# Top-10 indices of rows: a batch's store moved behind the last exponentials, quarter parts in shared buffers, ranks written into the table of the exactness test

One core of one Trainium2 chip. The metric is the device time of one execution in microseconds (us), lower is better.

## The reference

For each of 8192 rows of 8192 random numbers, the column indices of the ten largest, in falling order of value:

```python
def reference(x, k):                      # x: 8192 x 8192 float32, k = 10
    indices = np.argpartition(x, -k, axis=1)[:, -k:]
    values = np.take_along_axis(x, indices, axis=1)
    sorted_idx = np.argsort(-values, axis=1)
    return np.take_along_axis(indices, sorted_idx, axis=1)
```

## The kernel before

The rows are worked off in 64 tiles of 128 rows, 4 MB each. A tile goes through these stations:

1. *load* (SyncE's queue): four pieces of 1 MB; the first tile has eight and the last nine smaller ones.
2. *exponentials* (ScalarE): exp(36 (x - 4.7)) in bf16, in two halves; in four quarters for tiles 61 and 62; in eight parts for tile 63.
3. *sums* (TensorE, "s" in the profile): wide matmuls of 512 columns add the exponentials up in groups.
4. *choice* (VectorE, "wall" and "cidb"): the groups with the largest sums.
5. *gather* (GpSimd, "cand") and *mask* (half on GpSimd, half on VectorE, "masked"): the candidates of the chosen groups.
6. *extraction* (TensorE, "g"): 24 narrow fp32 matmuls a tile, 8 columns or (tiles 61 to 63) 16.
7. *rank* (VectorE, "t8a", "t8b", "posb").
8. For each batch of tiles *finish*: VectorE steps, then *moves* on TensorE ("fo"), a copy and a store.

The parts that matter here, with cuts marked:

```python
epool = ctx.enter_context(tc.tile_pool(name="e", bufs=3))      # exponentials
...
def part(h, s0, n):                                # one half or quarter of a tile
    e = epool.tile([P, N // 2], bf16, tag="e", name="e")   # always a whole buffer
    nc.scalar.activation(out=e[:, 0:n * W], in_=xts[t][:, s0 * W:(s0 + n) * W], ...)
    # ... n * W / 512 wide matmuls read e
...
for t in range(last - 1):                          # last = 63
    interleave(choose_steps(t), rank_steps(t - LAG) if t >= LAG else [])
    if t >= 1:
        spread(t - 1)                              # the masks
    gather(t, 0, G)
    if t < last - 2:
        run(weigh_steps(t + 1))                    # exponentials and sums
    if 1 <= t < last - 2:
        extract(t - 1)
    todo = {last - 5: 6, last - 4: TB, last - 3: TB}.get(t, 3)
    run(later[:todo])                              # steps of a batch's finish
    later = later[todo:]
    # ... a finished batch is added to `later`; load(t + 3)

a, b, c = last - 2, last - 1, last
run(later)
wb, wc = weigh_steps(b), weigh_steps(c)
run(wb[0:3])
extract(a - 1, 0, 6)
run(wb[3:4])
extract(a - 1, 6, G)
run(wc[0:4])
run(rank_steps(a - 2))
# ... masks of a, choice of b
extract(a, 0, 2)
run(wc[4:5])
extract(a, 2, 4)
run(wc[5:])
extract(a, 4, G)
run(rank_steps(a - 1))
# ... choice of c, extraction of b and c, ranks, two finishes, exactness test
```

Each engine works its instructions off in this order. A finish of batch 6 (seven tiles) is seven moves, 14 matmuls; they come before tile 61's sums in TensorE's order.

Of the kernel before, what the change touches and what calls it, by code (L numbers as in the profile page):

```python
# [1 line left out]

# [1 line left out]

# [5 lines left out]
P = 128  # L11
N = 8192
BANK = 512
KMAX = 10
G = 12
TB = 8
BETA = 36.0
# [3 lines left out]
BIG_NEG = -1e30  # L21
LAG = 3
TAIL = 3
PAD = 320



# [8 lines left out]
def kernel(  # L36
# [6 lines left out]
    nc = tc.nc  # L43
# [3 lines left out]
    ntiles = nrows // P  # L47

    fp32 = mybir.dt.float32
    fp16 = mybir.dt.float16  # L50
    bf16 = mybir.dt.bfloat16
# [5 lines left out]
    ACTF = mybir.ActivationFunctionType  # L57
# [5 lines left out]
    consts = ctx.enter_context(tc.tile_pool(name="consts", bufs=1))  # L63
    epool = ctx.enter_context(tc.tile_pool(name="e", bufs=3))
    small = ctx.enter_context(tc.tile_pool(name="small", bufs=2))
    bpool = ctx.enter_context(tc.tile_pool(name="batch", bufs=1))

    pad = ctx.enter_context(tc.tile_pool(name="pad", bufs=1)).tile([P, PAD], fp32, name="pad")
    nc.vector.memset(pad[:, 0:1], 0.0)
# [12 lines left out]
    last = ntiles - 1  # L82
# [5 lines left out]
    xts, ss, gs, idxs, cands, masked, batch = {}, {}, {}, {}, {}, {}, {}  # L88
    picked, ready = {}, {}

    def layout(t):
        return thin if t >= ntiles - TAIL else wide
# [8 lines left out]
    def parts(t):  # L101
        S = layout(t).S
        if t < ntiles - TAIL:
            return [S // 2] * 2
        return [S // 4] + [S // 8] * 5 + [S // 16] * 2 if t == last else [S // 4] * 4
# [25 lines left out]
    bias = consts.tile([P, 1], fp32)  # L131
# [3 lines left out]
    for lay, nsend in ((wide, TB), (thin, TAIL)):  # L135
        R, A, S = lay.R, lay.A, lay.S
# [8 lines left out]
        for s in range(S):  # L145
            nc.vector.tensor_copy(
                out=lay.group[:, s, :].rearrange("p (a s) -> p a s", s=S)[:, :, s],
                in_=lay.own_a,
# [8 lines left out]
    slots = consts.tile([P, G], fp16)  # L157
    nc.vector.tensor_copy(out=slots, in_=slots_i)
    wall = consts.tile([P, ntiles, 16], fp32)
    tall = consts.tile([P, ntiles], fp32)  # L160
    first_sum = np.cumsum([0] + [len(parts(t)) for t in range(ntiles)]).tolist()
    nsums = first_sum[-1]
    eall = consts.tile([P, nsums], fp32)
# [5 lines left out]
    def weigh_steps(t):  # L169
        lay = layout(t)  # L170
        S, W = lay.S, lay.W
        ss[t] = spsum.tile([P, wide.W], fp32, tag="s", name="s")[:, 0:W]

        def part(h, s0, n):
            e = epool.tile([P, N // 2], bf16, tag="e", name="e")
            nc.scalar.activation(  # L176
                out=e[:, 0:n * W], in_=xts[t][:, s0 * W:(s0 + n) * W],
                func=ACTF.Exp, bias=bias[:, 0:1], scale=BETA,
                accum_out=eall[:, first_sum[t] + h:first_sum[t] + h + 1],
            )  # L180
            for i in range(n):
                for j in range(0, W, BANK):
                    nc.tensor.matmul(sums[:, j:j + BANK], lhsT=lay.group[:, s0 + i, :],  # L183
                                     rhs=e[:, i * W + j:i * W + j + BANK],
                                     start=s0 + i == 0, stop=s0 + i == S - 1)

        sums, steps, s0 = ss[t], [], 0
        for h, n in enumerate(parts(t)):
            steps.append(lambda h=h, s0=s0, n=n: part(h, s0, n))
            s0 += n  # L190
        return steps
# [35 lines left out]
    def gather(t, g0, g1):  # L227
        if g0 == 0:
            cands[t] = small.tile([P, G, 16], fp32, tag="cand", name="cand")
        nc.gpsimd.add_instruction(  # L230
            mybir.InstIndirectCopy(
                name=nc.get_next_instruction_name(),
                ins=[nc.gpsimd.lower_ap(xts[t]), nc.gpsimd.lower_ap(idxs[t][:, g0:g1])],
                outs=[nc.gpsimd.lower_ap(cands[t][:, g0:g1].rearrange("p g s -> p (g s)"))],
                num_valid_indices=16 * (g1 - g0),
            )
        )
        if g1 == G:
            del xts[t], idxs[t]
# [15 lines left out]
    def spread(t):  # L255
        mask(nc.vector, t, 0, G // 2)
        mask(nc.gpsimd, t, G // 2, G)

    def extract(t, c0=0, c1=G):
        if c0 == 0:  # L260
            gs[t] = gpsum.tile([P, G * thin.R], fp32, tag="g", name="g")
        R = layout(t).R
        for c in range(c0, c1):
            nc.tensor.matmul(gs[t][:, c * R:(c + 1) * R],  # L264
                             lhsT=masked[t][:, c, :, :].rearrange("p a s -> p (a s)"),
                             rhs=layout(t).place, start=True, stop=True)

    def rank_steps(t):
        n = G * layout(t).R
        g = gs.pop(t)[:, 0:n]  # L270
        b = batch_of[t]
        pos = batch[b][1][:, t - starts[b], :]
        t8a = small.tile([P, 8], fp32, tag="t8a", name="t8a")
        t8b = small.tile([P, 8], fp32, tag="t8b", name="t8b")
        g2 = small.tile([P, G * thin.R], fp32, tag="g2", name="g2")[:, 0:n]
        return [
            lambda: nc.vector.max(out=t8a, in_=g),  # L277
            lambda: nc.vector.match_replace(out=g2, in_to_replace=t8a, in_values=g,  # L278
                                            imm_value=BIG_NEG),
            lambda: nc.vector.max_index(out=pos[:, 0:8], in_max=t8a, in_values=g),  # L280
            lambda: nc.vector.max(out=t8b, in_=g2),  # L281
            lambda: nc.vector.max_index(out=pos[:, 8:16], in_max=t8b, in_values=g2),  # L282
            lambda: nc.vector.tensor_copy(out=tall[:, t:t + 1],
                                          in_=t8b[:, KMAX - 9:KMAX - 8]),
        ]


# [67 lines left out]
        ]  # L355

    def interleave(*lists):
        for group_ in zip(*[l for l in lists if l]):
            for step in group_:
                step()  # L360

    def run(steps):
        for step in steps:
            step()

    good = consts.tile([P, nsums + ntiles], fp32)
    e10 = consts.tile([P, ntiles], fp32)
    with tc.manual_schedule():
        run(weigh_steps(0))
        later = []  # L370
        for t in range(last - 1):
            interleave(choose_steps(t), rank_steps(t - LAG) if t >= LAG else [])
            if t >= 1:
                spread(t - 1)
            gather(t, 0, G)
            if t < last - 2:
                run(weigh_steps(t + 1))
            if 1 <= t < last - 2:
                extract(t - 1)
            todo = {last - 5: 6, last - 4: TB, last - 3: TB}.get(t, 3)  # L380
            run(later[:todo])
            later = later[todo:]
            done = t - LAG
            if done >= 0 and batch_of[done] != batch_of[done + 1]:
                later += finish_steps(batch_of[done])
            if t + 3 < ntiles:
                load(t + 3)


        a, b, c = last - 2, last - 1, last  # L390
        run(later)
        wb, wc = weigh_steps(b), weigh_steps(c)
        run(wb[0:3])
        extract(a - 1, 0, 6)
        run(wb[3:4])
        extract(a - 1, 6, G)
        run(wc[0:4])
        run(rank_steps(a - 2))
        mask(nc.gpsimd, a, G // 2, G)
        run(choose_steps(b))  # L400
        mask(nc.vector, a, 0, G // 2)
        extract(a, 0, 2)
        run(wc[4:5])
        extract(a, 2, 4)
        run(wc[5:])
        extract(a, 4, G)
        run(rank_steps(a - 1))
        steps = finish_steps(batch_of[a - 1])
        run(steps[:4])
        mask(nc.gpsimd, b, G // 2, G)  # L410
        chosen = choose_steps(c)
        run(chosen[:4])
        mask(nc.vector, b, 0, G // 2)
        run(chosen[4:])
        extract(b)
        run(steps[4:7])
        mask(nc.vector, c, 0, G // 2)
        extract(c, 0, G // 2)
        nc.vector.tensor_scalar(
            out=good[:, 0:nsums], in0=eall, scalar1=FINITE, scalar2=None, op0=ALU.is_lt,  # L420
        )
        run(rank_steps(a))
        mask(nc.vector, c, G // 2, G)
        extract(c, G // 2, G)
        run(steps[7:])
        run(rank_steps(b))
        run(rank_steps(c))


        nc.scalar.activation(out=e10, in_=tall, func=ACTF.Exp, bias=bias[:, 0:1], scale=BETA)  # L430
        final = finish_steps(batch_of[last])
        run(final)
        nc.vector.scalar_tensor_tensor(
            out=good[:, nsums:nsums + ntiles], in0=e10, scalar=SLACK, in1=wall[:, :, G],
            op0=ALU.mult, op1=ALU.is_gt,
        )
# [10 lines left out]
    with tc.If(passed < checks):  # L447
        with tc.For_i(0, ntiles, 1) as i:
# [14 lines left out]
                out=out_u32[bass.ds(i * P, P), :], in_=o.rearrange("p k two -> p (k two)")  # L463
# [36 lines left out]
```

## Time and profile before

| | before |
|---|---|
| median of the first three executions | 679.84 us (679.68 to 680.17) |
| the traced execution | 682.78 us, of which 681.0 lie between its first and last instruction (its span) |
| loads | 268.58 MB at about 420 GB/s |
| busy: TensorE, VectorE, ScalarE | 81%, 82%, 73% |

Shares of busy time say little here, since the loads limit the time to about 640 us and everything else can only matter behind them. The times at which the last tiles pass the stations are what to read.

### The profile page before, as it was taken

To read this page: it belongs to the slowest core of one execution; us is meant where nothing else is said; L and a number is where in the kernel's file an instruction comes from. 1 tells how busy PE (TensorE), PEld (TensorE's weight loads), DVE (VectorE), ACT (ScalarE), POOL (GpSimd) and SP (SyncE) were. 2 spreads that over 40 slices of the span, in tenths; PEclk is the share of its full clock that TensorE was granted. 3 is DMA by queue.
4 is the path that set the end of the run, shared out by engine and by line. 5 is a ranking of instruction groups with operands and counts; after the bars stand their busy time and mean duration, and the time that the engine had idled before them with its cause. 6 is when DMAs were issued, how large, how long until landed. Compare 5 with 4: busy or idle time off the path is not lost. (4 is left out here: it accounts for less than half of the span.)

```text
span 681.0 us, 8025 instructions
## 1 busy us (share of the span) xinstructions
PE 552.1 (81%) x2690; PEld 342.3 (50%) x2690; DVE 556.2 (82%) x1336; ACT 494.9 (73%) x295; POOL 181.0 (27%) x136
## 2 busy tenths in 40 slices
PE   1587887879788888777887889698988888878987
PEld 0144544546544555444554555454555566545666
DVE  2576788789868987889877898879978897889786
ACT  4777777777777777767777777677677777778552
POOL 0113223313322322331331313331332232232240
PEclk9877677877966888788787597876688876876775
DMA  9999999999999999999999999999999999999900
GB/s 360 420 422 420 420 420 418 421 419 421 419 421 420 419 420 420 421 418 422 420 421 419 421 419 421 419 420 421 419 422 419 420 419 421 418 419 382 370 29 7
DMA packets 73713, 269.78 MB, mean 396 GB/s; under 512 B 4398, under 2 KB 5062, under 8 KB 73670
## 3 DMA queue, kind: packets, MB, share of 16 engines
q1 hardware_dynamic: 72976, 268.54, 96.7%
q10 hardware_dynamic: 694, 0.71, 0.3%
q8 instruction: 21, 0.34, 0.2%
q14 instruction: 22, 0.18, 0.1%
HBM read 268.58 MB, written 0.66 MB: 395 GB/s over the span
## 5 line engine op out<-in xcount | busy, mean ns | idle before, releaser
L176 ACT ACTIVATE e<-xt,bias 128x4096 bf16<-128x4096 f32 (+2 forms) x138 | 477.5, 3460 | 157.4 <-DMA xt<-in_x_dram 141.6
L183 PE MATMUL s<-e,group 128*128 128x512 bf16 x1024 | 339.9, 493 | 121.4 <-ACT e L176 121.3
L183 PEld LDWEIGHTS <-group 128*128 128x128 bf16 x1024 | 121.7, 122 | 311.9 <-issue 256.1
L264 PEld LDWEIGHTS g<-cpack,masked 128*128 128x128 f32 x1536 | 209.4, 216 | 19.0 <-issue 8.6
L264 PE MATMUL g<-cpack,masked 128*128 128x8 f32 (+1 forms) x1536 | 201.0, 270 | 2.6 <-DVE masked L247 2.6
L230 POOL INDIRECT_COPY cand<-xt,idx 128x192 f32 (+1 forms) x66 | 66.7, 1010 | 479.5 <-DMA xt<-in_x_dram 196.3
L217 DVE MAX8 wall<-s 128x8 f32<-128x1024 f32 (+1 forms) x64 | 77.2, 1207 | 114.1 <-PE s L183 113.9
L247 POOL TENSOR_TENSOR masked<-cand,cpack 128x768 f32<-128x768 f32 x63 | 113.4, 1800 | 5.2
L218 DVE FIND_INDEX8 cidb<-wall,s 128x8 uint16<-128x1024 f32 (+1 forms) x64 | 76.6, 1197 | 0.0
L223 DVE FIND_INDEX8 cidb<-wall,m 128x8 uint16<-128x1024 f32 (+1 forms) x64 | 76.4, 1193 | 0.0
L220 DVE MATCH_REPLACE8 m<-wall,s 128x1024 f32<-128x1024 f32 (+1 forms) x64 | 76.0, 1188 | 0.0
L222 DVE MAX8 wall<-m 128x8 f32<-128x1024 f32 (+1 forms) x64 | 75.7, 1184 | 0.2
L247 DVE TENSOR_TENSOR masked<-cand,cpack 128x768 f32<-128x768 f32 x65 | 61.6, 948 | 0.0
L330 PE MATMUL fo<-rows,send 128*64 128x160 f32 (+3 forms) x128 | 28.4, 374 | 1.1 <-DVE rows L314 1.1
L176 ACT ACTIVATION_READ_ACCUMULATOR e<-xt,bias 128x1 f32 x138 | 25.7, 186 | 0.0
L330 PEld LDWEIGHTS fo<-rows,send 128*64 128x64 f32 (+2 forms) x128 | 18.9, 164 | 3.7 <-DVE rows L314 1.7
L277 DVE MAX8 t8a<-g 128x8 f32<-128x96 f32 (+1 forms) x64 | 16.1, 252 | 1.7 <-PE g L264 1.7
L280 DVE FIND_INDEX8 posb<-t8a,g 128x8 uint16<-128x96 f32 (+1 forms) x64 | 16.6, 260 | 0.0
L282 DVE FIND_INDEX8 posb<-t8b,g 128x8 uint16<-128x96 f32 (+1 forms) x64 | 16.4, 256 | 0.0
L278 DVE MATCH_REPLACE8 g<-t8a,g 128x96 f32<-128x96 f32 (+1 forms) x64 | 16.1, 252 | 0.0
L281 DVE MAX8 t8b<-g 128x8 f32<-128x96 f32 (+1 forms) x64 | 15.8, 247 | 0.0
L209 DVE TENSOR_SCALAR idx<-cidb,cpack 128x12 uint16<-128x12 uint16 (+1 forms) x66 | 14.7, 223 | 0.2
(39 smaller groups left out, 94.7 us busy)
## 6 DMA issues: line engine op xcount, KB each, us to landing
xt<-in_x_dram SPq DMA_DIRECT2D x248, 1024.0 KB, 16.3
xt<-in_x_dram SPq DMA_DIRECT2D x15, 512.0 KB, 9.2
xt<-in_x_dram SPq DMA_DIRECT2D x2, 256.0 KB, 7.5
out_dram<-opack ACTq DMA_DIRECT2D x6, 80.0 KB, 5.3
cpack<-topk_cpack ACTq DMA_DIRECT2D x1, 141.0 KB, 3.3
out_dram<-opack ACTq DMA_DIRECT2D x1, 70.0 KB
out_dram<-opack SPq DMA_DIRECT2D x1, 60.0 KB, 1.7
out_dram<-opack SPq DMA_DIRECT2D x1, 30.0 KB, 1.4
```

Of the source, the lines that this page charges most:

```text
L176: nc.scalar.activation(out=e[:, 0:n * W], in_=xts[t][:, s0 * W:(s0 + n) * W], func=ACTF.Exp, bias=bias[:, 0:1], scale=BETA, accum_out=eall ...
L183: nc.tensor.matmul(sums[:, j:j + BANK], lhsT=lay.group[:, s0 + i, :], rhs=e[:, i * W + j:i * W + j + BANK], start=s0 + i == 0, stop=s0 + i ...
L217: lambda: nc.vector.max(out=w16[:, 0:8], in_=m),
L218: lambda: nc.vector.max_index(out=cid[:, 0:8], in_max=w16[:, 0:8], in_values=m),
L220: lambda: nc.vector.match_replace(out=m2, in_to_replace=w16[:, 0:8], in_values=m, imm_value=-1.0),
L222: lambda: nc.vector.max(out=w16[:, 8:16], in_=m2),
L223: lambda: nc.vector.max_index(out=cid[:, 8:16], in_max=w16[:, 8:16], in_values=m2),
L230: nc.gpsimd.add_instruction(mybir.InstIndirectCopy(name=nc.get_next_instruction_name(), ins=[nc.gpsimd.lower_ap(xts[t]), nc.gpsimd.lower_a ...
L247: eng.tensor_tensor(out=masked[t][:, g0:g1], in0=cands[t][:, g0:g1].unsqueeze(2).to_broadcast(shape), in1=layout(t).own.rearrange("p (c s) ...
L264: nc.tensor.matmul(gs[t][:, c * R:(c + 1) * R], lhsT=masked[t][:, c, :, :].rearrange("p a s -> p (a s)"), rhs=layout(t).place, start=True, ...
L280: lambda: nc.vector.max_index(out=pos[:, 0:8], in_max=t8a, in_values=g),
L330: nc.tensor.matmul(fo, lhsT=lay.send[:, i, 0:n * S], rhs=rows[:, i].rearrange("p a k -> p (a k)"), start=i == 0, stop=i == n - 1)
```

## The change

Its intent is to take a wait of 6.9 us off ScalarE. Two quarters of a tile share one exponential buffer. Three of the seven moves come before tile 61's sums and four after. The copy and the store of that batch move back, the store behind the last exponentials in ScalarE's order. All of tile 63's sums come before tile 61's extraction. A rank writes its second eight values straight into the table of the exactness test, which saves a copy per tile. Cut to its core:

```diff
-PAD = 320
+PAD = 256
-    tall = consts.tile([P, ntiles], fp32)
+    tall = consts.tile([P, ntiles, 8], fp32)
...
         def part(h, s0, n):
-            e = epool.tile([P, N // 2], bf16, tag="e", name="e")
+            at = s0 % (S // 2) * W
+            if at == 0:
+                half[0] = epool.tile([P, N // 2], bf16, tag="e", name="e")
+            e = half[0][:, at:at + n * W]
...
-        t8b = small.tile([P, 8], fp32, tag="t8b", name="t8b")
+        t8b = tall[:, t, :]
...
-            lambda: nc.vector.tensor_copy(out=tall[:, t:t + 1],
-                                          in_=t8b[:, KMAX - 9:KMAX - 8]),
...
-            todo = {last - 5: 6, last - 4: TB, last - 3: TB}.get(t, 3)
+            todo = {last - 5: 6, last - 4: 4, last - 3: 4, last - 2: 0}.get(t, 3)
...
-        run(later)
         wb, wc = weigh_steps(b), weigh_steps(c)
...
         run(wc[0:4])
+        run(later[:1])                    # the copy
         run(rank_steps(a - 2))
...
-        extract(a, 0, 2)
-        run(wc[4:5])
-        extract(a, 2, 4)
-        run(wc[5:])
-        extract(a, 4, G)
+        run(wc[4:])
+        run(later[1:])                    # the store
+        extract(a)
```

(`interleave` also learns lists of unequal length, since a rank has one step less.)

More of the change, by code (lines that the diff above doesn't have):

```diff
@@ L2 @@
 from contextlib import ExitStack
+from itertools import zip_longest
 import numpy as np
@@ L174, in part @@
         def part(h, s0, n):
-            e = epool.tile([P, N // 2], bf16, tag="e", name="e")
+            at = s0 % (S // 2) * W
+            if at == 0:
+                half[0] = epool.tile([P, N // 2], bf16, tag="e", name="e")
+            e = half[0][:, at:at + n * W]
             nc.scalar.activation(
-                out=e[:, 0:n * W], in_=xts[t][:, s0 * W:(s0 + n) * W],
+                out=e, in_=xts[t][:, s0 * W:(s0 + n) * W],
                 func=ACTF.Exp, bias=bias[:, 0:1], scale=BETA,
@@ L185, in part @@
                                      start=s0 + i == 0, stop=s0 + i == S - 1)
-        sums, steps, s0 = ss[t], [], 0
+        sums, half, steps, s0 = ss[t], [None], [], 0
         for h, n in enumerate(parts(t)):
@@ L357, in interleave @@
     def interleave(*lists):
-        for group_ in zip(*[l for l in lists if l]):
+        for group_ in zip_longest(*lists):
             for step in group_:
-                step()
+                if step:
+                    step()
     def run(steps):
@@ L427 @@
         run(rank_steps(c))
-        nc.scalar.activation(out=e10, in_=tall, func=ACTF.Exp, bias=bias[:, 0:1], scale=BETA)
+        nc.scalar.activation(out=e10, in_=tall[:, :, KMAX - 9], func=ACTF.Exp, bias=bias[:, 0:1], scale=BETA)
         final = finish_steps(batch_of[last])
```

## The prediction

> **What bounds the kernel now.** The page comes first. Its row of DMA digits is full up to slice 38, and the kernel reads 268.58 MB at about 420 GB/s, which alone is 639 us. In the steady part the exponentials wait for loads. A cost that is removed there buys nothing; only the tail, from about 623 us to the end at 681.0, can move.
>
> ```profile
> DMA  9999999999999999999999999999999999999900
> GB/s 360 420 422 420 420 420 418 421 419 421 419 421 420 419 420 420 421 418 422 420 421 419 421 419 421 419 420 421 419 422 419 420 419 421 418 419 382 370 29 7
> ```
>
> Next, the view of waits for 560 to 681 us and, for the loads' queue, for 640 to 650. Columns: who waited for whom, us in total, times, longest.
>
> ```profile
> ACT e L176 <- PE s L183: 6.9, 1, 6.9
> ...
> SPq L114 <- DMA out_dram<-opack: 3.9, 1, 3.9
> ```
>
> The first line is one stall. Tile 61 has four quarter parts, each takes a whole one of three exponential buffers, so its fourth needs the first one's matmuls done. Those stand behind 24 extraction matmuls and the 14 matmuls of the seven moves of batch 6. The timeline (start, length, engine, what, idle before):
>
> ```profile
> 628.22 2.00 ACT L176 ACTIVATE e<-xt,bias 128x2048 bf16<-128x2048 f32 x1 [0.46 <-DMA xt<-in_x_dram]
> ...
> 631.98 3.98 PE L330 MATMUL fo<-rows,send 128*56 128x160 f32 x14
> ...
> 635.89 2.96 PE L183 MATMUL s<-e,group 128*128 128x512 bf16 x12
> ...
> 637.21 2.00 ACT L176 ACTIVATE e<-xt,bias 128x2048 bf16<-128x2048 f32 x1 [6.90 <-PE s L183]
> 637.26 0.60 ACTq L353 DMA_DIRECT2D out_dram<-opack  x1
> ```
>
> From 637.21 on the scalar engine runs nearly back to back to 657.2; it is late, not waiting for data. The second line of waits is the store issued at 637.26: a later piece of the last tile's load reuses its landing semaphore and is issued at 641.81 instead of about 637.9.
>
> Last, the chain that ended last, in order of time (start, length, what). It is TensorE and VectorE, not the scalar engine:
>
> ```profile
> 647.25 1.24 PE g L264 x12
> 648.49 0.89 PE s L183 x4
> ...
> 649.40 0.71 DVE wall L217
> ...
> 654.25 0.86 DVE masked L247
> ...
> 655.25 0.59 PE g L264 x4
> ...
> 658.08 13.47 PE g L264 x64
> 671.54 3.38 PE fo L330 x12
> ```
>
> Tile 62's last sums (649.38) start VectorE's choice for it; the mask of tile 61 then starts the extraction. VectorE has no idle time from 649.40 to 669.9, and TensorE none from 655.25 to 674.9. They are almost tied: VectorE waits 1.67 us at 671.58 for the last extraction.
>
> **What the Trainium skill says.** "ScalarE: Activation LUTs", section "What ACT_TABLE_LOAD costs", gives an activation with a bias operand as about 280 ns + 0.833 ns per element: 1990 at 2048 elements. The trace has 1991, so parts that share a buffer cost what they cost now. "TensorE: Matmul & The Clock Gate", section "Part 1: The HAM clock gate", says that the clock is half or full, decided in free-running windows of about 3.4 us by recent activity. The trace agrees: the granted clock is 0.5 from 619 to 636, 1.0 to 643, 0.5 to 646.6, 1.0 to 656.8, then 0.5 to the end. 24 extraction matmuls take 2.74 us at full clock (640.22) and 5.12 at half (626.93). "DMA: Bandwidth & Descriptors", section "Why a DMA increments its semaphore by 16 and not by 1", says that up to 16 engines finish independently and only the full count means landed. It fits here: DMA busy share falls to 0.44 in 642 to 643, yet the landings keep their pace (below).
>
> **The change, part by part.**
>
> *Copies.* 64 copies of 128x1 at 142 ns go: 9.1 us of VectorE time. 61 lie beside DMA-bound work: nothing. In the tail the copies of tiles 60 to 63 cost about 0.11 us each in start-to-start time, of which one lies before the extraction of tile 62. The exponential at the end reads with a stride, 64 elements, 0.35 us, off the path.
>
> *Loads.* Moving the store behind the last exponentials takes away the 3.9 us wait. But pieces issued at 636.65 took 10.9 us to land (647.6), and the last, issued at 643.83, about 7.6 (651.4). That is 3.8 us for the last 1.5 MB, what 410 GB/s needs. The slowest DMA engine was never out of work, so I count 0 to 0.3 us and leave the last landing at 651.4.
>
> *Scalar engine.* Two quarters share a buffer, so three buffers hold six quarters. The fourth quarter starts when its piece has landed, about 630.8. Tile 62's pieces land from 633.2 to 640.9 (issued 619.45 to 627.35, 13.4 to 13.8 us each), so its parts end by 643.1 instead of 647.1. Tile 63's parts follow the landings: the last two, 0.72 us each, end at about 653.1 instead of 657.1. I assume that the second quarter's write does not wait for matmuls that read the first half of the same buffer: now, a mask of half of the candidates starts at 664.25, before the gather that fills the other half (665.70), so waits follow regions.
>
> *TensorE.* After extraction of tile 58 (ends 632.0) come three moves, six matmuls of 0.284 us (3.98/14) at half clock: 633.7. Then tile 61's 16 matmuls: six at 0.43 to 636.3, ten at 0.225 with full clock: 638.6 instead of 640.38. The extraction of tile 59 takes 2.74: 641.3. The four moves left, eight at about 0.14: 642.5. Now the clock decides. Before, it fell at 643:
>
> ```profile
> 642.00:643.00 1.00, 1.00 (x10) 0.91 (x10) 1.00 (x6) 1.00 (x1) 0.00 (x0) 1.00 0.44 166
> 643.00:644.00 1.00, 1.00 (x4) 0.39 (x3) 1.00 (x5) 1.00 (x3) 0.00 (x0) 0.57 0.90 320
> ```
>
> (after the stretch: PE, PEld, DVE, ACT and POOL busy, granted clock, DMA share, GB/s). The window before that fall was mostly narrow extraction, with about 0.9 us of wide matmuls. After the change it holds about 1.9 us of moves and sums. The window from 646.6 to 650 held about 1.2 and stayed full, so I give 65% to a clock that stays. Then tile 62's first 12 matmuls end at 645.2, half an extraction at 646.6, the last four at 647.5: 1.9 us before today's 649.38. If the clock falls as now, they end at about 649.2, 0.2 us earlier.
>
> *VectorE and the end.* From that start to the choice for tile 63 VectorE is dense (649.40 to 658.11), with one copy inside: the choice starts at 658.11 - 1.9 - 0.1 = 656.1. Tile 63's sums end at 653.4, so no new wait there. The mask of tile 62, which ends at 660.74 today, ends at 658.7. Tile 61's extraction, now unbroken by tile 63's sums, starts at about 653.4, runs at about 0.13 us a matmul while the clock is full, and is done by 657. So the extraction of tile 62 starts with its mask, at 658.7 instead of the 661.4 that 658.08 + 16 x 0.21 gives today. Then 48 matmuls at 0.211 (13.47/64), 10.1 us: 668.8 instead of 671.54, a gain of 2.7. Masks of tile 63 come about 2 us earlier too and stay ahead. The rest (ranking 1.9 us, final steps, the readback) is as before. In the other clock case the mask ends at 660.4 and extraction at 670.5: a gain of 1.0. Weighted, 0.65 x 2.7 + 0.35 x 1.0 = 2.1; I add 0.3 for a clock that in some executions stays full into tile 62's extraction. Predicted: 679.84 - 2.4 = 677.4.
>
> **Rivals.**
>
> 1. *The scalar engine is the bound, and its 6.9 us come off whole:* 673. For it: it runs back to back from 637 on. Against it: landings bound it at 651.4, so it gains only 4.0, and at 658.11 VectorE starts tile 63's choice without any wait at all, TensorE having ended the sums at 658.07. Four us less on one of two tied conditions cannot give four.
>
> 2. *Only the ordering moves, and the tail is bound by TensorE's half clock:* 679 to 680. TensorE's work is unchanged; the four moves now stand ahead of tile 62's sums, about 1.2 us, where they delay 649.38. For it: the tail from 655.25 is solid TensorE. Against it: TensorE stood idle from 653.5 to 655.25, and six matmuls of tile 63 were spliced into the extraction.
>
> 3. *Sharing makes a false dependence:* each second quarter waits for the matmuls of the first, or the new buffer addresses (the pad and the table move the x buffers by 1.5 KB) disturb something. The fourth quarter would then still stand behind TensorE, up to 638 us, and the time would be 679 to 682. Against it: waits by region, as said, and an activation in the same engine order has no other new partner.
>
> **Range and chances.** 1.0 and 2.7 us are the two clock cases; the free-running windows shift both by about a microsecond, and a full clock through all of the extraction would give about 4. So 676.0 to 679.1. 2% is 13.6 us, more than anything in the tail could give: faster 0.01, within 2% 0.985, slower 0.005.
>
> **What would show it.** Right: no wait of an exponential for TensorE near 630; no wait of the loads for the store near 640, and the last landing still near 651; scalar work ends near 653; TensorE has the wide matmuls done near 653.5; VectorE's choice for tile 62 starts near 647.5 with the clock full at 643 to 646; last extraction ends near 669. Wrong: if the last landing moves by more than 0.5 us; if quarter parts wait for TensorE; if the choice for tile 62 still starts at 649; or if a wait for a GpSimd gather opens before a mask of tile 62 or 63.

## The result, and the profile after

| | before | after |
|---|---|---|
| executions | 679.68, 680.17, 679.84, 678.47 | 680.31, 678.57, 679.64, 678.17 |
| median | 679.76 us | 679.11 us |
| ratio | | 0.9995, interval 0.9972 to 1.0017: the same |
| traced execution, span | 681.0 us | 678.5 us |

Ratios are the mean time of one kernel's fast runs over that of the other's of the same rounds, so they are not quite the ratio of the medians that are quoted. 679.11 lies just outside the predicted 676.0 to 679.1, and the gain of 0.65 in the medians is a quarter of the 2.4 predicted. Yet the two spans differ by 2.5. So two questions stand: did the tail change as predicted, and why do the timed executions not show it?

First the waits after the change, for 560 to 681 us (columns as in the prediction):

```profile
ACT e L181 <- DMA xt<-in_x_dram: 18.8, 18, 2.1
...
DVE t8a L282 <- PE g L269: 3.2, 1, 3.2
...
ACT e L181 <- PE s L188: 0.6, 1, 0.6
```

The wait of 6.9 us for TensorE has shrunk to 0.6; the exponentials wait for loads. VectorE's wait for the last extraction has grown from 1.7 to 3.2 us. Next, the timeline after (start, length, engine, what, count, idle before):

```profile
628.64 1.13 PE L333 MATMUL fo<-rows,send 128*56 128x160 f32 x6
...
629.70 4.95 PE L188 MATMUL s<-e,group 128*128 128x512 bf16 x15
...
630.58 2.00 ACT L181 ACTIVATE e<-xt,bias 128x2048 bf16<-128x2048 f32 x1 [0.40 <-DMA xt<-in_x_dram]
...
644.04 0.70 DVE L222 MAX8 wall<-s 128x8 f32<-128x512 f32 x1 [1.03 <-PE s L188]
...
652.51 0.71 ACT L181 ACTIVATE e<-xt,bias 128x512 bf16<-128x512 f32 x1
...
653.74 15.38 PE L269 MATMUL g<-cpack,masked 128*128 128x16 f32 x72
653.98 0.70 DVE L222 MAX8 wall<-s 128x8 f32<-128x512 f32 x1 [1.72 <-PE s L188]
...
669.15 0.37 DVE L282 MAX8 t8a<-g 128x8 f32<-128x192 f32 x1 [3.23 <-PE g L269]
```

The choice for tile 62 starts at 644.04 (before: 649.40), that for tile 63 at 653.98 (before: 658.11). These are gains of 5.4 and 4.1 us. But the last extraction, 72 matmuls without a gap, takes 15.38 us and ends at 669.12 instead of 671.54. So 1.7 of the 4.1 us are lost there. From here to the last instruction both kernels need 9.4 to 9.5 us. ScalarE's last part ends at 653.2 instead of 657.1.

What differs most between the two traces is the clock. This is the table of stretches; after the stretch come PE, PEld, DVE, ACT and POOL busy, then the granted clock, DMA share and GB/s. Before:

```profile
622.70:636.20 13.50, 12.64 (x47) 9.35 (x47) 11.38 (x27) 6.98 (x8) 2.81 (x2) 0.50 1.03 390
...
653.80:668.80 15.00, 13.55 (x66) 12.73 (x67) 14.55 (x46) 6.67 (x24) 5.16 (x5) 0.60 0.00 1
```

After:

```profile
622.70:636.20 13.50, 11.94 (x68) 7.78 (x68) 12.91 (x30) 12.15 (x13) 2.81 (x2) 0.87 1.05 408
...
653.80:668.80 15.00, 15.00 (x73) 15.00 (x71) 11.52 (x32) 3.88 (x16) 3.23 (x4) 0.50 0.00 1
```

Before, TensorE ran at half clock through all of 622.7 to 636.2, just where the stall arises, and got 47 matmuls done; after, 68 at 0.87. The change did not ask for that: in TensorE's order the kernels differ from the moves on (628.64 after), and the clocks part before, at 622.6. In the last stretch it is the other way round: half clock throughout after, 0.60 before.

### The profile page after: what moved, and what is told of

Read it like the earlier page. It is cut to its first block, busy times and chain, and to the rows that moved or that the text cites. A ratio compares the mean times of both kernels' runs of the same rounds, so it can differ in the third digit from the quotient of the medians.

```text
span 678.5 us, 7906 instructions
## 1 busy us (share of the span) xinstructions
PE 549.6 (81%) x2645; PEld 343.8 (51%) x2690; DVE 552.9 (81%) x1272; ACT 495.3 (73%) x295; POOL 180.0 (27%) x136
## 4 chain that ended last, share of the span: by engine, by line
DMA 61%; PE 12%; SPq 7%; ACT 7%; issue 5%; DVE 5%; POOL 3%; ACTq 0%; DVEq 0%
DMA xt<-in_x_dram 59%; SPq L115 7%; ACT e L181 7%; PE s L188 6%; PE g L269 5%; POOL cand L235 3%; DMA out_dram<-opack 2%; DVE wall L222 1%; PE fo L333 1%; DVE cidb L228 1%; DVE cidb L223 1%; DVE m L225 1%; DVE wall L227 1%; DVE masked L252 0%; DVE pick L350 0%
## 5 line engine op out<-in xcount | busy, mean ns | idle before, releaser
L188 PE MATMUL s<-e,group 128*128 128x512 bf16 x979 | 334.6, 496 | 122.1 <-ACT e L181 117.6
L285 DVE FIND_INDEX8 posb<-t8a,g 128x8 uint16<-128x96 f32 (+1 forms) x64 | 16.7, 260 | 0.0
L287 DVE FIND_INDEX8 posb<-tall,g 128x8 uint16<-128x96 f32 (+1 forms) x64 | 16.4, 257 | 0.0
L286 DVE MAX8 tall<-g 128x8 f32<-128x96 f32 (+1 forms) x64 | 15.8, 247 | 0.0
```

Source lines behind the costliest of these rows:

```text
L188: nc.tensor.matmul(sums[:, j:j + BANK], lhsT=lay.group[:, s0 + i, :], rhs=e[:, i * W + j:i * W + j + BANK], start=s0 + i == 0, stop=s0 + i ...
```

## The experiments

**Theories.** *A:* the traces are fair; the change gives 2.5 us and the timed executions scatter around that. *B:* the traced execution of before was a slow draw: the clock's free-running windows fell so that the half clock lasted from 619 to 636 us; most executions are not like it. *C:* after the change the half clock of the last 72 matmuls sets the end.

**The stand-in.** GpSimd's gather may not be used in new kernels. In each experiment it is replaced by a copy of the indices, iotas as filler, and a copy of as many elements, with the same dependences. Results are wrong, and the exactness test is made to pass always, at the same cost. So an experiment is compared with the same order under the stand-in; the true kernel before ran beside all of them.

```diff
-        nc.gpsimd.add_instruction(mybir.InstIndirectCopy(...))
+        fill = pad.bitcast(i32)
+        nc.gpsimd.tensor_copy(out=fill[:, 0:g1 - g0], in_=idxs[t][:, g0:g1])
+        for _ in range({12: 10, 6: 6}[g1 - g0]):       # s0 runs: 6 and 3
+            nc.gpsimd.iota(fill[:, 0:256], pattern=[[1, 256]], base=0, channel_multiplier=0)
+        nc.gpsimd.tensor_copy(out=cands[t][:, g0:g1]..., in_=xts[t][:, 16 * g0:16 * g1])
...
-            out=good[...], in0=e10, scalar=SLACK, in1=wall[:, :, G], op0=ALU.mult, op1=ALU.is_gt,
+            out=good[...], in0=e10, scalar=0.0, in1=wall[:, :, G], op0=ALU.mult, op1=ALU.is_le,
```

**1. A first look at both orders.**

> Kernel before with a stand-in for the GpSimd gather (a small copy of the indices, iotas as filler, a copy of as many elements; results are wrong on purpose, and the exactness test is made to pass always). It has to show whether the stand-in keeps the tail: from the indices to the end of the stand-in about 5.3 us for 192 elements and 3.1 us for 96, span about 677 to 681. It is a second draw of the free-running clock for the order of before. Theory 1 (the traced execution of before was an unlucky draw: its clock was at half from 619 to 636, which made the stall of 6.9 us): a stall of the fourth quarter well under 6.9 us in this draw, and the last extraction ends near 669 to 670. Theory 2 (the stall is there in each execution and the change costs elsewhere what it gains): the stall is again 6 to 7 us and the last extraction ends near 671.5.

> Changed kernel with the same stand-in. Both theories: no stall of a quarter part for TensorE over 1 us, scalar work ends near 653.3, last extraction near 668 to 669. A span within 2 us of s0_before speaks for theory 1.

683.35 and 680.04 us, spans 681.6 and 678.3, against 677.60 for the true kernel before on that chip. The filler was too short (about 3.7 and 1.6 us), and was lengthened afterwards. The trace of the order of before shows the stall of 6.9 us once more, and half clock from 619.6 to 636.7. In these two expectations Theory 1 is what B says below, and Theory 2 says that each execution has the stall; this trace taken alone spoke for Theory 2, and so for a fair trace of before.

**2. Both orders with repeated timing, twice on two chips, and before a third time.** No edit but the stand-in.

> Order of before with the stand-in for the gather, filler lengthened to the gather's own 5.3 and 3.1 us. Theory A (the traced executions are fair, the change gives its 2.5 us, but the clock after 653 us scatters each execution by a few us): timed executions scatter by 2 us or more and s1_before is 2 to 3 us above s1_after in the mean. Theory B (the traced execution of before was a slow draw; most have no stall of 6.9 us): the timed executions lie 2 us or more under the traced one, and s1_before is at most 1 us above s1_after.

> Changed kernel with the same stand-in. Theory A: 2 to 3 us under s1_before. Theory B: 0 to 1 us under it, and its traced execution close to its timed ones.

> s1_before once more: six more executions, one more trace. Theory B (the traced execution of before, 681.0 us of span, was one of the slowest): most executions 677.5 to 681, at most one in six above 682; the mean within 1.2 us of s2_after. Theory A (a steady 2 to 3 us): mean 2 to 3 us above s2_after.

> s1_after once more. Theory B: mean near 679.2, and a narrower scatter than that of before, as no execution has the stall of a quarter part; its last extraction begins near 653 and takes 15 us unless the clock stays full past 655.

> The order of before a third time. Mean 680 to 681; with 18 executions, between one and four above 682. Its trace shows a stall of the fourth quarter between 4 and 7 us, the longer the more of 619 to 636 is at half clock.

| | executions | mean, standard error | lowest to highest |
|---|---|---|---|
| s1_before, s2_before, s5_before | 18 | 680.41 ± 0.34 | 677.54 to 683.51 |
| s1_after, s2_after | 12 | 679.04 ± 0.25 | 677.77 to 680.21 |
| true kernel before, all that ran beside (the four of the result among them) | 39 | 679.46 ± 0.19 | 677.39 to 683.06 |
| true kernel after | 4 | 679.17 ± 0.49 | 678.17 to 680.31 |

The traced 682.78 us is not among the 39, and only two of those are slower. This supports the first half of B: the base that the prediction reasoned from was a rare one. It is not the profiler that slows an execution: over the 17 kernels that were timed more than once with their trace among the times, the traced execution took 0.2 ± 0.3 us more than the mean of the others. The means under the stand-in differ by 1.4 ± 0.4 us, between B's "at most 1" and A's 2 to 3; of the true kernels by 0.3 ± 0.5. Scatter after is smaller, as B expected. The new traces of before have a shorter wait for TensorE, here s1_before and s5_before:

```profile
ACT e L178 <- PE s L185: 5.1, 1, 5.1
```

```profile
ACT e L178 <- PE s L185: 4.3, 1, 4.3
```

Between 619 and 636 us their clock was at half for 9 and 10 us, in two pieces each, against 17 in the traced before, and their spans are 678.7 and 677.8. Expected was a wait that grows with the half clock. Between these two it does not, but over all traces in which the fourth quarter still needs a buffer of its own behind all seven moves it does:

| half clock between 619 and 636 us | wait of the fourth quarter for TensorE |
|---|---|
| 0 (s4_before_warm, below) | 1.2 |
| 6.1 (s6_wc_table), 6.8 (s6_before_less) | 3.2, 2.4 |
| 9.3 (s1_before), 9.8 (s2_before), 10.2 (s5_before) | 5.1, 5.1, 4.3 |
| 16.4 (s0_before), 16.7 (before) | 6.9, 6.9 |

The clock changes only at multiples of 3.413 us from each other within an execution, and the place of these steps against the program is different in each. Of the 20 traces, those whose steps fall at 1.44 to 1.82 us (the remainder of the time after division by 3.4133; a range chosen after the traces were seen) are three: the traced before, s0_before, and s2_gap_wide below. All three had 17 us of half clock from 619 to 636. None of the others had.

**3. The parts alone.** Sharing alone is the diff of `part` above. The store part alone is the `todo` line, the removed `run(later)` and the two runs of `later`. The remaining parts are the order of tile 63's sums and the table.

> s1_before with one part of the change alone: quarter parts share buffers, order as before. Six quarters fit, so no stall of a quarter part for its buffer, the store is issued when the copy is done (near 636), and TensorE still does all seven moves before tile 61's sums. Theory A: 1 to 2 us under s1_before. Theory B: within 0.5 us of it.

> s1_before with the other part alone: three moves before tile 61's sums and four after, copy and store at the end, no sharing. A stall remains but ends when the first quarter's matmuls do, near 635 at half clock. Theory A: 1 to 2 us under s1_before; Theory B: within 0.5 us. The last load lands at the same time as in s1_before within 0.5 us though no load waits for the store.

> s1_store again. If the moved store and moves carry the change: mean of both within 0.5 us of s1_after and s2_after, 678.6 to 679.6.

> The order of before with the remaining parts: all of tile 63's sums before tile 61's extraction, and ranks that write into the table. The stall of the fourth quarter stays at 4 to 7 us and the mean within 0.7 us of the order of before, 679.8 to 680.8.

*Sharing alone:* 680.50 ± 0.36, no gain. Its wait has only changed hands. The waits of s1_share (2 waits, the longest 3.8 us):

```profile
ACT e L181 <- DVE opack L329: 5.7, 2, 3.8
```

The fourth quarter starts at 630.6, but the store comes next in ScalarE's order and waits for the copy, which waits for all seven moves; tile 62's first part starts at 636.5. That is what the title's first part is for.

*Store part alone:* 678.68 ± 0.43 in two sets, 12 executions, as good as the whole change (679.04 ± 0.25). In s1_store the fourth quarter waits only 0.5 us, for its load, even without sharing, where I expected a stall to about 635. Both traces had little half clock between 619 and 636 us, though (6.7 and 3.4). No load waits for the store, and the last landing is at 651.1 (s1_before: 651.5). One of the 12 took 682.94.

*Remaining parts alone:* 678.66 ± 0.48, 1.8 ± 0.6 us under the order of before (1.7 ± 0.8 under s5_before, on the same chip), where I expected at most 0.7: a miss. The trace still shows the wait, of 3.2 us (expected were 4 to 7), and the choice for tile 63 at 653.6. So parts of the change that leave the stall in place gain, within these errors, as much as the part that removes it. The gains don't add up: the whole gives 1.4.

**4. The half clock before the stall taken away.** Unread wide matmuls keep TensorE busy in tiles 58 to 60.

```diff
+    warm = ...tile_pool(name="warm", bufs=1, PSUM).tile([P, BANK], fp32)   # gpsum: 2 buffers, not 3
...  # at the end of part()
+            for _ in range({0: 6, 1: 2}[h] if last - 5 <= t <= last - 3 else 0):
+                nc.tensor.matmul(warm, lhsT=lay.group[:, s0, :], rhs=e[:, 0:512], start=True, stop=True)
```

> s2_before with 6 unread wide matmuls after the first half and 2 after the second half of tiles 58, 59 and 60 (written to a bank freed by giving the extraction two instead of three), which keep TensorE busy between 598 and 626 us. If the half clock makes the stall: the clock is at full for most of 619 to 636, the fourth quarter waits at most 2.5 us instead of 4.7 to 6.9, and the mean is at least 1 us under that of s1_before and s2_before (680.5). If matmul order and buffers alone make it: the stall stays at 4.5 us or more and the mean rises by the added work, to 681 or more.

> The same matmuls in s2_after. If the half clock is the cause of the scatter in before: this one gains at most 0.5 us on s1_after and s2_after (679.0) and lies within 0.8 us of s4_before_warm, so most of the change's gain is then gone. Otherwise it stays 1 to 2 us under s4_before_warm.

s4_before_warm 679.89 ± 0.52 (7 executions), s4_after_warm 678.87 ± 0.30. In the trace of the first, the longest wait is 1.5 us, and the clock is full in the stretch that was at half:

```profile
ACT e L179 <- PE s L186: 2.7, 2, 1.5
```

```profile
622.70:636.20 13.50, 11.15 (x70) 7.68 (x70) 13.02 (x31) 10.17 (x11) 9.37 (x17) 1.00 1.04 379
636.80:653.20 16.40, 15.39 (x61) 9.80 (x62) 11.56 (x36) 12.80 (x15) 12.92 (x30) 0.56 0.70 271
```

So the half clock makes the long stall: the order and the three exponential buffers are the same, and it is gone (the fourth quarter waits 1.2 us). But the expected 1 us or more did not come: 0.5 ± 0.6. This traced execution took 682.71 us without the long stall. The half clock came later, from 638.8 to 655.9, and ScalarE stood idle again, before 652.49 (put down to "issue"). The choice for tile 63 started at 657.9. The stall was one place in which a half clock can cost time, not the cost itself.

The edit also adds a wait of its own, since the extraction has two buffers instead of three: the last 24 matmuls wait for a rank.

```profile
652.49 1.15 ACT L179 ACTIVATE e<-xt,bias 128x1024 bf16<-128x1024 f32 x1 [2.84 <-issue]
...
666.25 5.27 PE L268 MATMUL g<-cpack,masked 128*128 128x16 f32 x24 [2.24 <-DVE posb L284]
```

In s4_after_warm this wait is 0.9 us. So the means of this experiment do not say what a full clock before 636 us is worth. s4_after_warm lies 1.0 ± 0.6 us under s4_before_warm, where at most 0.8 was expected if the half clock were the whole of the change's gain: undecided.

**5. The clock at the very end.** Unread wide matmuls in the gaps between tile 63's sums; as a control the same with 16 columns; then also one after each second extraction step.

```diff
...  # in part(), t == last; `full` is the whole sums tile, its second half is free
+                for _ in range({1: 2, 2: 2, 3: 2, 4: 2, 5: 2, 6: 1}.get(h, 0)):
+                    nc.tensor.matmul(full[:, W:W + w], lhsT=..., rhs=e[:, 0:w], start=True, stop=True)   # w = 512 or 16
...  # s3_gap_and_inner alone, in extract()
+            if t in (last - 2, last - 1, last) and c % 2 == 1:
+                spare[0](512)                          # one such matmul more
```

> s2_after with 11 wide matmuls of 512 columns, whose results nobody reads, in the gaps in which TensorE waits for tile 63's exponentials (about 647 to 652). Theory C (after the change the end is set by 72 extraction matmuls at half clock, 15.4 us against 9.4 at full): the last extraction begins at most 0.3 us later, the clock falls one window of 3.4 us later, and the mean is 1 to 1.5 us under s2_after. If TensorE's clock is not what counts: the same as s2_after or 0.3 us above.

> The control of s2_gap_wide: the same 11 matmuls with 16 columns instead of 512, so the same order and waits without the activity. Theory C: within 0.4 us of s2_after in the mean, the clock falls near 653 to 656.

> s2_gap_wide with one more unread wide matmul after each second extraction step of tiles 61, 62 and 63 (18 in all). If the half clock of the last extraction sets the end after the change: the clock stays full to about 665, the extraction ends 1 to 3 us earlier, near 666, and the mean is 1 us or more under s2_after (679.0). If VectorE's masks set it: VectorE's wait before the last ranking falls from 3.2 us toward 0 and the gain is under 1 us. If the added work only costs: up to 4 us slower.

678.93 ± 0.66 and 678.80 ± 0.19 (5 executions), against 678.90 ± 0.42 for s2_after on the same chip: no gain is seen, with an error of 0.8 us for the first against the 1 to 1.5 expected. The third took 683.36 ± 0.13, 4.3 us slower than the changed order: it is the only large effect, and it is pure cost. The timeline of TensorE in s2_gap_wide says why the clock did not help in that execution:

```profile
654.50 2.75 PE L277 MATMUL g<-cpack,masked 128*128 128x16 f32 x24
659.52 10.39 PE L277 MATMUL g<-cpack,masked 128*128 128x16 f32 x48 [2.27 <-DVE masked L260]
```

Tile 61's extraction ran at full clock, 0.115 us a matmul, in 2.75 us. Then TensorE waited 2.27 us for VectorE's mask of tile 62, and the 48 matmuls left ran at half clock, 0.216 each. In s3_gap_and_inner the same wait is 2.8 us, the clock falls in it at 659.5, and 12 of the 18 added matmuls then cost half-clock time. Here a full clock for the first third is given back as a wait for VectorE.

Two other traces say that it need not be. The mask of tile 62 in the traced after, and the last extraction in s2_after, whose clock fell only at 654.19:

```profile
655.65 0.95 DVE L252 TENSOR_TENSOR masked<-cand,cpack 128x768 f32<-128x768 f32 x1
```

```profile
652.74 14.21 PE L270 MATMUL g<-cpack,masked 128*128 128x16 f32 x72
```

In the first, the mask was ready at 656.6 and TensorE came to it at 658.9 (24 matmuls of 0.214 after 653.74); a faster first third would have been kept. In the second the 72 matmuls ended 2.2 us before those of the traced after. The trace of s2_gap_wide is the slowest of its six executions and one of the three with 17 us of half clock before 636, so VectorE was late in it. Theory C is neither borne out nor refuted.

**6. Less extraction.** Tile 61 in six steps of 32 columns instead of twelve of 16, 12 of the last 72 matmuls less (about 2.5 us at half clock); wrong results.

```diff
+        two = 2 if t == last - 2 else 1
-        for c in range(c0, c1):
-            nc.tensor.matmul(gs[t][:, c * R:(c + 1) * R], lhsT=..., rhs=layout(t).place, ...)
+        for c in range(c0, c1, two):
+            nc.tensor.matmul(gs[t][:, c * R:(c + two) * R], lhsT=...,
+                             rhs=layout(t).own[:, 0:two * R] if two == 2 else layout(t).place, ...)
```

(The table's exponential has scale 1 here, since sums of two rows' values would overflow.)

> s2_before with half of tile 61's extraction (6 steps of twice the columns instead of 12, so 12 of the 72 last matmuls less, about 2.5 us at half clock; wrong results). VectorE waits 1.5 to 1.7 us before the last ranking in the traces of the order of before, and the mask of tile 62 bounds the extraction behind it. If VectorE's chain bounds the end nearly as much: 0 to 1 us faster than s1, s2 and s5_before (680.4). If TensorE alone bounds it: 2 us or more faster.

> The same in s2_after, where VectorE waits 1.6 to 3.2 us before the last ranking. If TensorE's extraction bounds the end after the change: 1.5 to 2.5 us faster than s1_after and s2_after (679.0), so 676.5 to 677.5. If VectorE's chain does: less than 1 us.

679.43 ± 0.36, 1.0 ± 0.5 under before; 678.18 ± 0.33, 0.9 ± 0.4 under after. The work taken away is 2.5 us at half clock; in both traces tile 61's extraction ran at full clock, where it is 1.3 (12 matmuls of 32 columns in 1.42 us for 24 of 16 in 2.75, as in s0_after). So between a third and three quarters of it came through. In s6_after_less TensorE then waited 2.9 us for the mask of tile 62. In the traced after it did not wait there, but in s0_after it waited 2.6, without any work removed. So VectorE's chain stands close behind TensorE's, and which of them comes last differs from one execution to the next.

One more use of this run: the trace of s6_before_less has its clock steps 0.24 us from those of the traced before (622.42, 619.01 against 619.25), and at 622.4 its clock went up, where that of before stayed down:

```profile
622.70:636.20 13.50, 11.98 (x65) 7.90 (x66) 11.59 (x28) 10.44 (x11) 10.42 (x20) 0.87 1.04 396
```

Apart from the stand-in, nothing that this experiment edits comes before 640 us. Its stall is 2.4 us instead of 6.9, its span 676.0 instead of 681.0, of which the removed work explains at most 2.5, and at this trace's full clock 1.3. (That the stand-in moved the clock cannot be excluded, though s0_before, with a stand-in too, kept the half clock.)

## Why the prediction was wrong

What held, on the traced execution:

| step | predicted | traced |
|---|---|---|
| fourth quarter starts | 630.8 | 630.6 |
| tile 63's exponentials end | 653.1 | 653.2 |
| last load lands | 651.4, 0 to 0.3 earlier | 651.9 |
| choice for tile 62 starts | 647.5 | 644.0 |
| choice for tile 63 starts | 656.1 | 654.0 |
| last extraction starts, ends | 653.4, 668.8 | 653.7, 669.1 |
| change of the traced execution | -2.4 | 682.78 to 680.31: -2.5 |

The parts on loads and ScalarE held. The load's wait for the store is gone, as these lines show (the loads' queue; before it was 9.7 in all with 3.9 the longest), and it bought nothing, since the landings kept their pace: the last piece was issued at 642.15 instead of 643.83 and took 9.8 us instead of 7.6.

```profile
SPq L115 <- DMA out_dram<-opack: 4.7, 6, 1.4
```

**The step that failed is the last one: "Predicted: 679.84 - 2.4 = 677.4".** The 2.4 us were worked out for the execution in the trace, and subtracted from the median of others. The traced one took 682.78. Taken from there, 2.4 gives 680.4, and the traced execution after took 680.31. That the two agree is luck: 680.31 is the slowest of the four executions after, whose mean is 679.17. The executions that make up the median had less to lose, if they are like those of the stand-in: three of its four traces of this order have 9 to 10 us of half clock where the traced before has 17, and a stall of 4.3 to 5.1 instead of 6.9 (experiments 2 and 4). What the change takes off them is 0.3 ± 0.5 us between the true kernels, 1.4 ± 0.4 under the stand-in.

**Two terms of the sum were also mis-sized, in opposite directions.** "Six at 0.43 to 636.3" kept the clock of the traced before for the changed kernel. In the trace after it was full from 622.6 to 629.4 and from 632.8 on; the tile's sums ended at 634.7, not 638.6, and the choice for tile 62 came 3.5 us earlier than predicted. "About 0.13 us a matmul while the clock is full" for tile 61's extraction failed too: the clock fell at 653.3, just before that extraction began, and all 72 took 0.214 (15.38/72). Where the prediction had VectorE's mask of tile 62 as the bound, TensorE was; the two errors met at 668.8 and 669.1. So the agreement of the sum on the trace is partly luck. The 65% for "a clock that stays" between 643 and 646 came out as bet, but not by the reason given. The prediction took little wide matmul work in the window before for the cause of a fall. In the trace after, the window from 643.08 to 646.50 had 1.61 us of it and the clock stayed full; that from 649.90 to 653.32 had 1.75 and the clock fell. What makes it fall stays open. The windows that mattered more were before 636 and after 653, and beyond the 0.3 us added at the end I had not put a chance on them.

**The rivals.** "The scalar engine is the bound" fell: it is 3.9 us earlier and the end only 2.5. "Only the ordering moves" named the time, 679 to 680, by another reason: TensorE's half clock does bound the traced after, though the moves did not delay tile 62's sums. "Sharing makes a false dependence" fell: the second and third quarters in the trace start at 626.1 and 628.1 with no wait for TensorE.

**What stays open.** The true kernel before left one trace, so that its usual executions look like those of its stand-in is argued, not shown; the stand-in's mean is 0.95 ± 0.39 us above the true kernel's. Why the remaining parts alone gain 1.8 us, and why gains don't add, I can only argue: the end is the later of two chains a few us apart, and each execution draws its own clock for one of them.

No experiment gives a version that is clearly faster than both kernels. The store part alone matches the whole change within its error.

## What to carry to other kernels

Before a gain is read out of a trace, hold the traced execution's own time against the timed ones; if they differ by as much as the gain, the trace is one draw, and the gain belongs to that draw. A wait that is removed is worth only the slack to the next chain: here, between the two traces, four us of earlier work gave two and a half, and 1.3 to 2.5 us less matmul work gave one. An order that needs the clock in a certain state at a certain time should be judged by the mean and scatter of many executions.

## What the Trainium skill lacked or had wrong

- "TensorE: Matmul & The Clock Gate", section "Part 1: The HAM clock gate": it says that the clock follows how busy TensorE was in windows of about 3.4 us, and the steps here are multiples of 3.413 us. The section does not say what counts as busy. Here TensorE's instructions filled 15.00 of 15.00 us with narrow fp32 extraction, and 12.64 of 13.50 before, at a granted clock of 0.50. Busy time in the profile is not the activity that lifts the clock.
- The same section says that the windows run freely, so that the ramp varies from run to run, and that its penalty is under 1% of a typical kernel's span. It speaks of the ramp at the start, which no run here measures. Here the clock changes to the end of the kernel, and 39 executions of one kernel spread from 677.39 to 683.06 us, 0.8%; how much of that is the clock is not shown. What the section lacks is the warning that such a spread can be more than twice the gain that was predicted for a change, and that a single trace is then one draw: steps 0.24 us apart went with a stall of 2.4 and one of 6.9 us.
- No page has that filling TensorE's gaps with unread matmuls to hold the clock may not pay: 11 of them showed no gain (678.93 ± 0.66 against 678.90 ± 0.42 us), 29 cost 4.3 us.
- "DMA: Bandwidth & Descriptors" has nothing on a load that waits at issue for a store's semaphore while earlier loads are still in flight: removing 3.9 us of such a wait moved the last landing from 651.4 to 651.9, that is, not forward at all.
